# Loading the residual into the accumulator, a third pair of projection weight buffers, and layer norm cut into pieces between projection steps, in a hybrid SSD and MLP block

## The chip, the cores and the metric

The kernel runs on one core of one Trainium2 chip. The metric is the device time of one execution in microseconds (us); lower is better. The engines are named as in the profile: PE is TensorE (PEld its weight loads), DVE is VectorE, ACT is ScalarE, POOL is GpSimd, and SP is the engine whose queue issues the DMAs. One PSUM tile here is 128 partitions by 512 floats.

## The reference

One post-norm layer over 1040 positions (16 meta tokens and 1024 inputs) with 1024 channels. Cut to its last part, which the change touches:

```python
h = layer_norm(concat([meta, x]), ln_in_g, ln_in_b)
...
merged = sigmoid(g_ssm) * (y_ssm @ w_proj_ssm) + sigmoid(g_pool) * (y_pool @ w_proj_pool)
h = layer_norm(ALPHA * h + merged @ w_out, ln1_g, ln1_b)
a, v = split(h @ w_up)                                # 2816 columns each
f = (silu(causal_dwconv(a, conv_w, conv_b)) * v) @ w_down
h = layer_norm(ALPHA * h + f, ln2_g, ln2_b)
return h[:, 16:]
```

ALPHA is 2 to the power of 0.25. All tensors are float32.

## The kernel before

**Arithmetic.** Activations lie transposed, with channels on the partitions and positions in the free dimension. Each float32 operand is split in two by `split` (L117): a rounded copy `hi`, cast by ACT, and the remainder `lo = src - hi`, subtracted by POOL or DVE. A product is three matmuls (`mm3`, L144): hi by hi, hi by lo, lo by hi. A weight tile is 128 by 1024 floats: `loadw` (L128) loads it into `wraw` (two buffers), splits it into `whi` and `wlo` (two buffers each, in the pool `wp`), and the subtraction goes by turns to POOL and DVE in the stretch in question (`lo_pat`).

**The stages around the change, in program order.**

1. Branch projections. For each of eight row blocks m, `gemm(w_ps[m, :, 8:, :], ...)` (L686) multiplies four position chunks CQ (258, 256, 258 and 256 positions); `ev_ssm` (L664) loads the gate `gr` by DMA, multiplies it with the result, adds `acc[:, m]` and splits the sum into `mgh[i]` and `mgl[i]` of chunk i.
2. Output projection. `out_gemm(*idx)` (L712) runs over m and, inside, over the chunks in idx. For each product it loads a piece of the residual `hr` from `h_d` (one buffer) and computes `acc = ALPHA * hr + product` on DVE (L723). Chunks 0 and 2 go first, then 1, then 3.
3. First layer norm. `out_ln(i)` (L725) takes a chunk of `acc`: 86 or 128 positions at a time are transposed on PE into two PSUM tiles, statistics run on DVE (L177), the power of -0.5 on POOL (L184), the normalisation on ACT (L738); the result is transposed back on PE (L744), scaled by DVE and ACT (L746, L748) and written to `h1_d`.
4. `ops_lo` and `ops_hi` (L756, L760) build the operands B11, B21, B22 and T1 to T4 of a seven-product block multiplication from two halves of the positions, each as hi and lo. They overwrite `mgh` and `mgl` and fill `x3h` and `x3l`.
5. Up projection. For f from 0 to 21, `up_weights` (L801) builds weight sums from two `wraw` tiles, `up_steps` runs the seven products for the two subchunks, and `up_act` (L885) applies convolution, SiLU and product and writes `f_d[f]`. The tiles `fpre` and `fv` of even f lie in the pool `pe`, those of odd f in `p6`. The first two f are run in halves, since the second half of the positions is ready later.
6. Down projection. `f_load` (L919) loads `f_d[f]` into `fr`, splits it into `fh` and `fl`; blocks of f (`FBLK`, the first is 0 to 2) are multiplied with `w_down` and added to `acc`. The pool `fp` reuses the memory of `mgs`, `x3s` and `wxs`.
7. Last layer norm, by position chunks 2, 1, 0: transposes, statistics, normalisation on ACT (L1003), then multiply by g2 and add b2 (L1005, L1006) on DVE (a quarter of chunk 0 on POOL), and the output DMA.

**Order.** All instructions are laid out at build time by a scheduler that takes the ready instruction that comes first in the program; `tc.high_priority(offset=n)` moves a block n places forward. Each engine, SP's queue among them, then runs its list strictly in order, and waits at the head of its list. A tile's buffer is reused when all readers of its last content are done. `reuse_waits="tile"` keeps the waits for reused pool memory separate for each tile. `f_d` is one DRAM tile, so its loads and stores are ordered as a whole.

Of the kernel before, what the change touches and what calls it, by code (L numbers as in the profile page):

```python
# [14 lines left out]
P = 128  # L15
# [12 lines left out]
T0 = 12  # L28
# [42 lines left out]
def hybrid_block(ctx: ExitStack, tc, x, w_in, w_dt, pool_w, w_ps, w_pp, w_out, w_up, w_down,  # L71
# [23 lines left out]
    h1_d = dr.tile([KD, P, NT], F32, name="h1_d")  # L95
    f_d = dr.tile([NFF, P, SEQ], F32, name="f_d")
    ac_d = dr.tile([NC, NH, P], F32, name="ac_d")
# [587 lines left out]
    for m in range(KD):  # L685
        gemm(w_ps[m, :, 8:, :], KD, lambda k, a, b: (yb[k][0][:, a:b], yb[k][1][:, a:b]), CQ, ev_ssm(m, True))  # L686
    ybs.close()
    yrs.close()
# [20 lines left out]
    with tc.tile_pool(name="p5", bufs=2, side="right") as p5:  # L709
        hx = {}  # L710

        def out_gemm(*idx):  # L712
            for m in range(KD):
                w = loadw(w_out[m], 8)
                for i in idx:
                    a, b = CQ[i]
                    n = b - a
                    hx[i] = acc[:, :, a:b]
                    ps = gtile()[:, :n]
                    mm3(ps, w, 0, KD, lambda k, a, b: (mgh[i][:, k, :n], mgl[i][:, k, :n]), a, b)  # L720
                    hr = p5.tile([P, 258], F32, tag="hr", name="hr", bufs=1)
                    SY.dma_start(hr[:, :n], h_d[m, :, a + T0:b + T0])
                    V.scalar_tensor_tensor(hx[i][:, m, :], hr[:, :n], ALPHA, ps, ALU.mult, ALU.add)  # L723

        def out_ln(i):  # L725
# [5 lines left out]
            for o in range(0, n, st):  # L731
                pa = [stile("l0"), stile("l1")]
                for k in range(KD):
                    PE.transpose(pa[k // 4][:st, (k % 4) * P:(k % 4 + 1) * P], X[:, k, o:o + st], idn)
                rr = ln_stats(p5, [q[:st] for q in pa], st)
                xn = p5.tile([P, D], F32, tag="xn", name="xn", bufs=3)
                for q in range(2):
                    S.activation(xn[:st, 512 * q:512 * q + 512], pa[q][:st], AF.Identity,  # L738
                                 bias=rr[:st, 1:2], scale=rr[:st, 0:1])
                xs.append((xn, o))  # L740
            for k in range(KD):
                ps = stile("lb")
                for xn, o in xs:
                    PE.transpose(ps[:, o:o + st], xn[:st, k * P:(k + 1) * P], idn[:st, :st])  # L744
                if k % 2:
                    V.tensor_scalar(X[:, k, :n], ps[:, :n], col(PC_1G, k), col(PC_1B, k), ALU.mult, ALU.add)  # L746
                else:
                    S.activation(X[:, k, :n], ps[:, :n], AF.Identity, bias=col(PC_1B, k), scale=col(PC_1G, k))  # L748

            SY.dma_start(h1_d[:, :, a:b].rearrange("k p t -> p k t"), X)  # L750
# [33 lines left out]

        out_gemm(0, 2)
        out_ln(0)
        ops_lo(0)
        out_gemm(1)
        out_ln(2)
        ops_hi(0)  # L790
        out_ln(1)
        ops_lo(1)
        out_gemm(3)
        out_ln(3)
        ops_hi(1)
# [4 lines left out]
    with tc.tile_pool(name="p6", bufs=2, side="right", reuse_waits="tile") as p6:  # L800
# [104 lines left out]
        for f in range(2, NFF):  # L905
            o = up_outs(f)
            up_steps(up_weights(f), *o, [(j, s) for j in range(7) for s in range(2)])
            up_act(f, *o)
    wxs.close()
    x3s.close()  # L910
    mgs.close()
# [3 lines left out]
    fps = ExitStack()  # L915
    fp = fps.enter_context(tc.tile_pool(name="fp", bufs=1, reuse_waits="tile"))
    fops = {}

    def f_load(f):  # L919
        fr = fp.tile([P, SEQ], F32, tag="fr", name="fr", bufs=2)  # L920
        SY.dma_start(fr, f_d[f])
        x, n = ("e", 3) if f in FEARLY else ("", 7)
        th = fp.tile([P, SEQ], F32R, tag="fh" + x, name="fh", bufs=n)
        tl = fp.tile([P, SEQ], F32R, tag="fl" + x, name="fl", bufs=n)
        split(th, tl, fr, lo_eng=V if f < 3 else None)
        fops[f] = th, tl

    with tc.tile_pool(name="p7", bufs=2, reuse_waits="tile") as p6:
        g2 = p6.tile([P, D], F32, name="g2", bufs=1)
        b2 = p6.tile([P, D], F32, name="b2", bufs=1)  # L930
        for f in range(*FBLK[0]):
            f_load(f)
        SY.dma_start(g2, ln2_g.partition_broadcast(P))
        SY.dma_start(b2, ln2_b.partition_broadcast(P))

# [10 lines left out]
        for bi, (f0, f1) in enumerate(FBLK):  # L946
            K = f1 - f0
            fs = [fops.pop(f) for f in range(f0, f1)]
            if f1 < NFF:
                n0, n1 = FBLK[bi + 1]  # L950
                todo = list(range(n0, n1))
                for m in range(KD):
                    if todo:
                        f_load(todo.pop(0))
                    down(m, loadw(w_down[m, :, f0:f1, :], K), K, fs, list(enumerate(CD)), first=bi == 0)
        wcs = ExitStack()
        wcp = pool(wcs, "wcp", 1, side="right")
# [10 lines left out]
        for i in (2, 1, 0):  # L968
# [21 lines left out]
            for o in range(0, b - a, P):  # L990
# [6 lines left out]
                else:  # L997
                    st, pa = pas[o]
                    rr = ln_stats(p6, [], P, st)
                xn = p6.tile([P, D], F32, tag="sa", name="xn", bufs=2)  # L1000
                for q in range(2):
                    sl = slice(512 * q, 512 * q + 512)
                    S.activation(xn[:, sl], pa[q], AF.Identity, bias=rr[:, 1:2], scale=rr[:, 0:1])  # L1003
                    eng = G if i == 0 and o and q else V
                    eng.tensor_mul(xn[:, sl], xn[:, sl], g2[:, sl])  # L1005
                    eng.tensor_add(xn[:, sl], xn[:, sl], b2[:, sl])  # L1006
                    SY.dma_start(out[a + o:a + o + P, sl], xn[:, sl])
# [56 lines left out]
```

## Time and profile before

| | |
|---|---|
| median of 3 runs | 2085.41 us (2081.19 to 2085.63) |
| profiled execution | 2079.03 us |
| its span, first to last instruction | 2077.2 us |
| PE busy | 2002.1 us (96%) |
| DVE busy | 1088.8 us (52%) |
| ACT busy | 780.7 us (38%) |
| POOL busy | 704.1 us (34%) |
| DMA, mean over the span | 103 GB/s |

The profiled execution is 6.4 us below the median of the timed runs. Times in the rows are us from the start of the span. Matmul records overlap, since matmuls are pipelined: a record of 0.28 us can follow the one before by 0.12 us. PEclk 1.00 stands for 2.4 GHz and 0.50 for 1.2 GHz, the two levels of the granted clock.

### The profile page before, as it was taken

Reading aid. Unit: us, or ns where it says so; the run is one execution under the profiler, and the core shown is the slowest. Engines: PE = TensorE matmul, PEld = TensorE weight load, DVE = VectorE, ACT = ScalarE, POOL = GpSimd, SP = SyncE. Lnnn points to the kernel's source line nnn. Section 1 sums busy time; section 2 is a strip of 40 time slices with the busy share of each in tenths; the row PEclk is TensorE's granted clock in tenths of the full one; section 3 lists DMA queues with packets and bytes.
Section 4 is the critical chain, followed back from the end, with each engine's and each line's share of the span. In section 5 each row is a group of like instructions: output and inputs, shape, how many; then the busy total and the mean of one; then the engine's idle time right before and its main releaser. Section 6 shows DMA issues by size and latency. Waiting matters only on the chain.

```text
span 2077.2 us, 33694 instructions
## 1 busy us (share of the span) xinstructions
PE 2002.1 (96%) x13921; PEld 1926.7 (93%) x13921; DVE 1088.8 (52%) x1697; ACT 780.7 (38%) x1146; POOL 704.1 (34%) x447
## 2 busy tenths in 40 slices
PE   7999999999999999999999997889999999899997
PEld 6999999999999999999999997779999999778886
DVE  7847757757755223342233424775554645453337
ACT  4544544635534323232111214554444434322112
POOL 4046657557566310013242323432112121142101
PEclk9999999999999999999999999999999999999998
DMA  6122223232234342225433345452222222343212
GB/s 211 53 81 78 88 79 127 82 112 96 79 114 126 98 142 63 73 78 167 127 121 97 88 123 153 136 174 91 92 72 82 82 72 91 110 159 95 71 54 82
DMA packets 88177, 213.92 MB, mean 103 GB/s; under 512 B 10600, under 2 KB 40136, under 8 KB 88024
## 3 DMA queue, kind: packets, MB, share of 16 engines
q1 hardware_dynamic: 88024, 211.77, 32.1%
q8 instruction: 109, 1.79, 0.4%
q14 instruction: 44, 0.36, 0.1%
HBM read 170.38 MB, written 41.35 MB: 102 GB/s over the span
## 4 chain that ended last, share of the span: by engine, by line
PE 79%; DVE 8%; DMA 5%; POOL 4%; issue 2%; ACT 2%; SPq 0%; POOLq 0%; DVEq 0%; ACTq 0%
PE gps L113 71%; PE sps L113 3%; DMA hr<-h_d 3%; PE yd L113 1%; POOL acb L425 1%; DVE Ct L223 1%; POOL wlo L119 1%; PE yo L113 1%; DMA fr<-f_d 1%; DVE lnst L177 1%; PE st L113 1%; DVE wlo L119 1%; DMA wraw<-in_w_up 1%; DVE acb L426 1%; PE xt L433 1%
## 5 line engine op out<-in xcount | busy, mean ns | idle before, releaser
L113 PE MATMUL gps<-hh,whi 128*128 128x384 f32 (+2 forms) x1536 | 497.8, 324 | 1.1 <-ACT hh L282 1.1
L113 PE MATMUL gps<-hl,whi 128*128 128x384 f32 (+2 forms) x1536 | 493.6, 321 | 4.3 <-POOL hl L285 2.6
L113 PE MATMUL gps<-hh,wlo 128*128 128x384 f32 (+2 forms) x1536 | 490.3, 319 | 0.0
L118 ACT CAST whi<-wraw 128x1024 fp32r<-128x1024 f32 (+3 forms) x246 | 222.2, 905 | 614.8 <-PE gps L113 419.0
L119 POOL TENSOR_TENSOR wlo<-wraw,whi 128x512 fp32r<-128x512 f32 (+1 forms) x85 | 187.7, 2208 | 490.5 <-ACT whi L118 480.4
L113 PEld LDWEIGHTS gps<-hh,whi 128*128 128x128 f32 x1536 | 288.2, 188 | 8.4 <-issue 3.9
L113 PEld LDWEIGHTS gps<-hl,whi 128*128 128x128 f32 x1536 | 288.7, 188 | 7.4 <-POOL hl L285 4.8
L113 PEld LDWEIGHTS gps<-hh,wlo 128*128 128x128 f32 x1536 | 289.5, 189 | 0.8 <-issue 0.8
L119 DVE TENSOR_TENSOR wlo<-wraw,whi 128x1024 fp32r<-128x1024 f32 (+3 forms) x161 | 191.5, 1190 | 148.9 <-ACT whi L118 148.3
L113 PE MATMUL gps<-mgh,wlo 128*128 128x256 f32 (+1 forms) x784 | 225.0, 287 | 10.4 <-POOL wlo L119 7.2
L113 PE MATMUL gps<-mgh,whi 128*128 128x256 f32 (+1 forms) x784 | 224.3, 286 | 4.1 <-ACT whi L118 3.4
L113 PE MATMUL gps<-mgl,whi 128*128 128x256 f32 (+1 forms) x784 | 223.7, 285 | 0.0
L113 PEld LDWEIGHTS gps<-mgh,wlo 128*128 128x128 f32 x784 | 150.2, 192 | 13.0 <-POOL wlo L119 8.9
L113 PEld LDWEIGHTS gps<-mgh,whi 128*128 128x128 f32 x784 | 149.9, 191 | 5.4 <-ACT whi L118 4.5
L113 PE MATMUL gps<-x3h,wlo 128*128 128x258 f32 (+1 forms) x528 | 149.4, 283 | 2.3 <-DVE wlo L119 2.3
L113 PE MATMUL gps<-x3h,whi 128*128 128x258 f32 (+1 forms) x528 | 148.7, 282 | 1.9 <-ACT whi L118 0.9
L113 PEld LDWEIGHTS gps<-mgl,whi 128*128 128x128 f32 x784 | 150.1, 191 | 0.0
L113 PE MATMUL gps<-x3l,whi 128*128 128x258 f32 (+1 forms) x528 | 148.4, 281 | 0.2 <-DVE x3l L119 0.2
L113 PE MATMUL gps<-yh,whi 128*128 128x384 f32 (+3 forms) x448 | 133.6, 298 | 0.0
L113 PE MATMUL gps<-yh,wlo 128*128 128x384 f32 (+3 forms) x448 | 133.4, 298 | 0.0
L113 PE MATMUL gps<-yl,whi 128*128 128x384 f32 (+3 forms) x448 | 133.3, 298 | 0.0
L113 PE MATMUL gps<-fh,whi 128*128 128x512 f32 (+2 forms) x312 | 121.8, 392 | 10.2 <-ACT fh L118 10.2
(256 smaller groups left out, 4184.2 us busy)
## 6 DMA issues: line engine op xcount, KB each, us to landing
wraw<-in_w_in SPq DMA_DIRECT2D x64, 512.0 KB, 3.7
wraw<-in_w_up SPq DMA_DIRECT2D x48, 512.0 KB, 3.5
acb<-ac_d SPq DMA_DIRECT2D x32, 512.0 KB, 4.0
wraw<-in_w_out SPq DMA_DIRECT2D x24, 512.0 KB, 3.7
f_d<-sa SPq DMA_DIRECT2D x22, 512.0 KB, 2.6
fr<-f_d SPq DMA_DIRECT2D x22, 512.0 KB, 3.3
y_d<-xy SPq DMA_DIRECT2D x16, 514.0 KB, 4.2
yr<-y_d SPq DMA_DIRECT2D x16, 514.0 KB, 3.6
```

The costliest lines, as they stand in the source:

```text
L113: PE.matmul(ps, lhsT, rhs, start=start, stop=stop, **kw)
L118: (S.copy if hi_eng is None else hi_eng)(hi, src)
L119: (G if lo_eng is None else lo_eng).tensor_sub(lo, src, hi.bitcast(F32))
L177: V.bn_stats(st[:n, i, :], p)
L223: V.scalar_tensor_tensor(dst, pre[:, j:j + T], cw(j), dst, ALU.mult, ALU.add)
L425: G.tensor_tensor(sg, sg, acc_[:L, c, h0:h1, None].to_broadcast([L, HPG, L]), ALU.subtract)
L426: V.tensor_scalar(sg, sg, 0.0, None, ALU.min)
L433: PE.transpose(px[:L, j * P:(j + 1) * P], xy[:, j, a:b], idn)
```

## The change

The residual is loaded into `acc[:, m]` by one DMA per m right after the last branch projection of m, in place of 32 loads of `hr`; the accumulation reads and writes `acc` in place. The weights of the output projection rotate over three pairs of `whi` and `wlo`, the third in the pool `wx` (its tag is also that of the third pair of the up projection); one subtraction in three goes to POOL and two to DVE. `out_gemm` and `out_ln` become generators, and a written order interleaves the projection steps of chunks 1 and 3 with pieces of the norms of chunks 0, 2 and 1; the norm of chunk 3 comes at the end. `f_d` becomes 22 DRAM tiles. The first three `f_load` calls get a high priority, with their operands in a new pool `fpe` that is opened once `mgs` is closed; the first two load into the memory of `fpre` and `fv` of even f. The loads of g2 and b2 move behind the down projection's first four blocks. In the last layer norm's last chunk, two fused DVE instructions per half replace ACT's normalisation and the multiplication and addition; the mean is taken as it is, without the product with the power (`raw=True`).

```diff
--- before.py
+++ after.py
@@ -93,7 +93,7 @@
     sg_d = dr.tile([KD, P, NT], F32, name="sg_d")
     sp_d = dr.tile([KD, P, NT], F32, name="sp_d")
     h1_d = dr.tile([KD, P, NT], F32, name="h1_d")
-    f_d = dr.tile([NFF, P, SEQ], F32, name="f_d")
+    f_d = [dr.tile([P, SEQ], F32, name=f"f_d{f}") for f in range(NFF)]
     ac_d = dr.tile([NC, NH, P], F32, name="ac_d")
     ea_d = dr.tile([NC, 2, 16, P], F32, name="ea_d")
     rs_d = dr.tile([NG, NT], F32, name="rs_d")
@@ -684,6 +684,7 @@
         mgl.append(mgp.tile([P, KD, 258], F32R, name=f"mgl{i}"))
     for m in range(KD):
         gemm(w_ps[m, :, 8:, :], KD, lambda k, a, b: (yb[k][0][:, a:b], yb[k][1][:, a:b]), CQ, ev_ssm(m, True))
+        SY.dma_start(acc[:, m, :], h_d[m, :, T0:])
     ybs.close()
     yrs.close()
 
@@ -709,18 +710,32 @@
     with tc.tile_pool(name="p5", bufs=2, side="right") as p5:
         hx = {}
 
+        slot = [0]
+
+        def out_w(m):
+            j = slot[0] % 3
+            slot[0] += 1
+            with tc.high_priority(offset=WPRI):
+                raw = wp.tile([P, KD, P], F32, tag="wraw", name="wraw")
+                SY.dma_start(raw, w_out[m])
+                pl, sfx = (wx, "x") if j == 2 else (wp, "")
+                hi = pl.tile([P, KD, P], F32R, tag="whi" + sfx, name="whi")
+                lo = pl.tile([P, KD, P], F32R, tag="wlo" + sfx, name="wlo")
+                split(hi, lo, raw, lo_eng=G if j == 1 else V)
+            return hi, lo
+
         def out_gemm(*idx):
             for m in range(KD):
-                w = loadw(w_out[m], 8)
+                w = out_w(m)
                 for i in idx:
                     a, b = CQ[i]
                     n = b - a
                     hx[i] = acc[:, :, a:b]
                     ps = gtile()[:, :n]
                     mm3(ps, w, 0, KD, lambda k, a, b: (mgh[i][:, k, :n], mgl[i][:, k, :n]), a, b)
-                    hr = p5.tile([P, 258], F32, tag="hr", name="hr", bufs=1)
-                    SY.dma_start(hr[:, :n], h_d[m, :, a + T0:b + T0])
-                    V.scalar_tensor_tensor(hx[i][:, m, :], hr[:, :n], ALPHA, ps, ALU.mult, ALU.add)
+                    o = hx[i][:, m, :]
+                    V.scalar_tensor_tensor(o, o, ALPHA, ps, ALU.mult, ALU.add)
+                yield
 
         def out_ln(i):
             a, b = CQ[i]
@@ -738,6 +753,7 @@
                     S.activation(xn[:st, 512 * q:512 * q + 512], pa[q][:st], AF.Identity,
                                  bias=rr[:st, 1:2], scale=rr[:st, 0:1])
                 xs.append((xn, o))
+                yield
             for k in range(KD):
                 ps = stile("lb")
                 for xn, o in xs:
@@ -746,7 +762,8 @@
                     V.tensor_scalar(X[:, k, :n], ps[:, :n], col(PC_1G, k), col(PC_1B, k), ALU.mult, ALU.add)
                 else:
                     S.activation(X[:, k, :n], ps[:, :n], AF.Identity, bias=col(PC_1B, k), scale=col(PC_1G, k))
-
+                if k % 4 == 3:
+                    yield
             SY.dma_start(h1_d[:, :, a:b].rearrange("k p t -> p k t"), X)
 
         def osplit(name, s, src, lo_eng):
@@ -782,16 +799,32 @@
             V.tensor_sub(t4, xb, t2)
             osplit("T4", s, t4, V)
 
-        out_gemm(0, 2)
-        out_ln(0)
+        def run(g, n=99):
+            for _ in range(n):
+                if next(g, g) is g:
+                    break
+
+        run(out_gemm(0, 2))
+        g1, g3 = out_gemm(1), out_gemm(3)
+        l0, l1, l2, l3 = (out_ln(i) for i in range(4))
+        for todo in ((l0, l0), (l0,), (), (l0,), (l0, l2), (l2,), (l2,), ()):
+            run(g1, 1)
+            for l in todo:
+                run(l, 1)
+        run(l0)
         ops_lo(0)
-        out_gemm(1)
-        out_ln(2)
+        run(g3, 1)
+        run(l2, 1)
+        run(g3, 1)
+        run(l2)
         ops_hi(0)
-        out_ln(1)
+        for todo in ((l1,), (l1,), (l1,), (), (l1,), (l1,)):
+            run(g3, 1)
+            for l in todo:
+                run(l, 1)
+        run(l1)
         ops_lo(1)
-        out_gemm(3)
-        out_ln(3)
+        run(l3)
         ops_hi(1)
 
 
@@ -906,32 +939,36 @@
             o = up_outs(f)
             up_steps(up_weights(f), *o, [(j, s) for j in range(7) for s in range(2)])
             up_act(f, *o)
+    mgs.close()
+
+
+    lo_pat["p"] = (V,)
+    fps = ExitStack()
+    fpe = fps.enter_context(tc.tile_pool(name="fpe", bufs=1, reuse_waits="tile"))
+    fops = {}
+
+    def f_load(f, fr=None):
+        if fr is None:
+            fr = fpe.tile([P, SEQ], F32, tag="fr", name="fr", bufs=2)
+        SY.dma_start(fr, f_d[f])
+        pl, x, n = (fpe, "e", 3) if f in FEARLY else (fp, "", 7)
+        th = pl.tile([P, SEQ], F32R, tag="fh" + x, name="fh", bufs=n)
+        tl = pl.tile([P, SEQ], F32R, tag="fl" + x, name="fl", bufs=n)
+        split(th, tl, fr, lo_eng=V if f < 3 else None)
+        fops[f] = th, tl
+
+    with tc.high_priority(offset=600):
+        for f in range(2):
+            f_load(f, pe.tile([P, NT], F32, tag=("fpre", "fv")[f], name="fre", bufs=1)[:, :SEQ])
     wxs.close()
     x3s.close()
-    mgs.close()
-
-
-    lo_pat["p"] = (V,)
-    fps = ExitStack()
     fp = fps.enter_context(tc.tile_pool(name="fp", bufs=1, reuse_waits="tile"))
-    fops = {}
-
-    def f_load(f):
-        fr = fp.tile([P, SEQ], F32, tag="fr", name="fr", bufs=2)
-        SY.dma_start(fr, f_d[f])
-        x, n = ("e", 3) if f in FEARLY else ("", 7)
-        th = fp.tile([P, SEQ], F32R, tag="fh" + x, name="fh", bufs=n)
-        tl = fp.tile([P, SEQ], F32R, tag="fl" + x, name="fl", bufs=n)
-        split(th, tl, fr, lo_eng=V if f < 3 else None)
-        fops[f] = th, tl
 
     with tc.tile_pool(name="p7", bufs=2, reuse_waits="tile") as p6:
         g2 = p6.tile([P, D], F32, name="g2", bufs=1)
         b2 = p6.tile([P, D], F32, name="b2", bufs=1)
-        for f in range(*FBLK[0]):
-            f_load(f)
-        SY.dma_start(g2, ln2_g.partition_broadcast(P))
-        SY.dma_start(b2, ln2_b.partition_broadcast(P))
+        with tc.high_priority(offset=600):
+            f_load(2)
 
         def down(m, w, K, fs, chunks, first=False):
             for i, (a, b) in chunks:
@@ -953,6 +990,8 @@
                     if todo:
                         f_load(todo.pop(0))
                     down(m, loadw(w_down[m, :, f0:f1, :], K), K, fs, list(enumerate(CD)), first=bi == 0)
+        SY.dma_start(g2, ln2_g.partition_broadcast(P))
+        SY.dma_start(b2, ln2_b.partition_broadcast(P))
         wcs = ExitStack()
         wcp = pool(wcs, "wcp", 1, side="right")
         wc = {m: loadw(w_down[m, :, f0:f1, :], K) for m in range(2)}
@@ -996,14 +1035,18 @@
                     rr = ln_stats(p6, pa, P)
                 else:
                     st, pa = pas[o]
-                    rr = ln_stats(p6, [], P, st)
+                    rr = ln_stats(p6, [], P, st, raw=True)
                 xn = p6.tile([P, D], F32, tag="sa", name="xn", bufs=2)
                 for q in range(2):
                     sl = slice(512 * q, 512 * q + 512)
+                    if i == 0:
+                        V.scalar_tensor_tensor(xn[:, sl], pa[q], rr[:, 1:2], g2[:, sl], ALU.subtract, ALU.mult)
+                        V.scalar_tensor_tensor(xn[:, sl], xn[:, sl], rr[:, 0:1], b2[:, sl], ALU.mult, ALU.add)
+                        SY.dma_start(out[a + o:a + o + P, sl], xn[:, sl])
+                        continue
                     S.activation(xn[:, sl], pa[q], AF.Identity, bias=rr[:, 1:2], scale=rr[:, 0:1])
-                    eng = G if i == 0 and o and q else V
-                    eng.tensor_mul(xn[:, sl], xn[:, sl], g2[:, sl])
-                    eng.tensor_add(xn[:, sl], xn[:, sl], b2[:, sl])
+                    V.tensor_mul(xn[:, sl], xn[:, sl], g2[:, sl])
+                    V.tensor_add(xn[:, sl], xn[:, sl], b2[:, sl])
                     SY.dma_start(out[a + o:a + o + P, sl], xn[:, sl])
         wcs.close()
     fps.close()
```

## Rows read from the trace of the kernel before

**Rows 1.** Stretches: length, busy us (instructions) of PE, PEld, DVE, ACT, POOL; PEclk, DMA.

```profile
1100.00:1201.00 101.00, 101.00 (x826) 101.00 (x826) 39.42 (x74) 21.01 (x39) 28.76 (x35) 1.00 0.35 94
1201.00:1247.10 46.10, 46.10 (x387) 46.10 (x386) 11.32 (x21) 8.81 (x9) 10.18 (x5) 1.00 0.42 124
1247.10:1327.50 80.40, 65.91 (x526) 63.06 (x523) 49.55 (x86) 42.06 (x53) 35.50 (x20) 0.96 0.56 166
1327.50:1394.50 67.00, 52.14 (x358) 47.41 (x358) 48.47 (x67) 33.41 (x52) 22.55 (x12) 0.92 0.46 157
1394.50:1795.00 400.50, 400.24 (x3358) 400.08 (x3358) 218.44 (x322) 170.80 (x301) 72.60 (x40) 1.00 0.24 80
1795.00:1809.70 14.70, 4.42 (x10) 2.98 (x10) 5.67 (x6) 3.94 (x5) 0.00 (x0) 0.66 0.62 205
1809.70:2063.60 253.90, 251.14 (x1202) 211.79 (x1201) 118.93 (x182) 53.89 (x70) 50.98 (x25) 1.00 0.29 93
```

**Rows 2.** Waits of PE, 1247.1 to 1327.5: us in total, times, longest.

```profile
PE l L734 <- ACT xn L738: 6.8, 2, 5.3
PE lb L744 <- ACT xn L738: 3.0, 3, 1.9
PE gps L113 <- POOL wlo L119: 2.4, 3, 1.2
PE gps L113 <- DVE wlo L119: 1.5, 2, 0.8
PE gps L113 <- ACT whi L118: 0.7, 1, 0.7
```

**Rows 3.** Waits of PE, 1327.5 to 1394.5.

```profile
PE gps L113 <- POOL wlo L119: 4.5, 4, 1.7
PE gps L113 <- DVE wlo L119: 4.0, 5, 1.1
PE gps L113 <- ACT whi L118: 3.5, 3, 1.6
```

**Rows 4.** Timeline of DVE: start, duration, instruction, in brackets idle before and releaser.

```profile
1233.50 1.22 DVE L119 TENSOR_TENSOR wlo<-wraw,whi 128x1024 fp32r<-128x1024 f32 x1
...
1252.32 0.42 DVE L723 SCALAR_TENSOR_TENSOR acc<-hr,gps 128x258 f32<-128x258 f32 x1 [4.80 <-DMA hr<-h_d]
...
1305.03 2.49 DVE L119 TENSOR_TENSOR wlo<-wraw,whi 128x1024 fp32r<-128x1024 f32 x1
...
1338.05 0.42 DVE L723 SCALAR_TENSOR_TENSOR acc<-hr,gps 128x256 f32<-128x256 f32 x1 [0.84 <-DMA hr<-h_d]
```

**Rows 5.** Timeline of PE, first product of the up projection.

```profile
1328.68 0.39 PE L113 MATMUL gps<-mgh,wlo 128*128 128x258 f32 x1 [1.23 <-POOL wlo L119]
```

**Rows 6.** Waits of all engines, 1100 to 1201.

```profile
DVE gr L667 <- PE gps L113: 53.3, 31, 3.8
```

**Rows 7.** Chain that ended last, 1770 to 1830, in order of time.

```profile
1777.90 2.89 PE sps L113 x24
...
1798.94 0.33 SPq L894
...
1799.79 5.63 DMA fr<-f_d
```

**Rows 8.** Timelines of DVE and PE around the start of the down projection.

```profile
1778.63 1.23 DVE L893 TENSOR_TENSOR sa<-sa,fv 128x1024 f32<-128x1024 f32 x1
...
1805.29 1.22 PE L113 MATMUL gps<-fh,whi 128*128 128x512 f32 x2 [10.24 <-ACT fh L118]
...
1809.70 0.44 PE L113 MATMUL gps<-fh,whi 128*128 128x512 f32 x1
```

**Rows 9.** Timeline of DVE at the end.

```profile
2066.08 0.27 DVE L181 TENSOR_SCALAR lnmv<-lnmv 128x1 f32<-128x1 f32 x2
...
2068.03 1.36 DVE L1005 TENSOR_TENSOR xn<-xn,g 128x512 f32<-128x512 f32 x2 [0.38 <-ACT xn L1003]
...
2072.30 1.63 DVE L1006 TENSOR_TENSOR xn<-xn,b 128x512 f32<-128x512 f32 x1
```

More of the change, by code (lines that the diff above doesn't have):

```diff
@@ L908, in hybrid_block @@
             up_act(f, *o)
-    wxs.close()
-    x3s.close()
     mgs.close()
@@ L915, in hybrid_block @@
     fps = ExitStack()
-    fp = fps.enter_context(tc.tile_pool(name="fp", bufs=1, reuse_waits="tile"))
+    fpe = fps.enter_context(tc.tile_pool(name="fpe", bufs=1, reuse_waits="tile"))
     fops = {}
-    def f_load(f):
-        fr = fp.tile([P, SEQ], F32, tag="fr", name="fr", bufs=2)
+    def f_load(f, fr=None):
+        if fr is None:
+            fr = fpe.tile([P, SEQ], F32, tag="fr", name="fr", bufs=2)
         SY.dma_start(fr, f_d[f])
-        x, n = ("e", 3) if f in FEARLY else ("", 7)
-        th = fp.tile([P, SEQ], F32R, tag="fh" + x, name="fh", bufs=n)
-        tl = fp.tile([P, SEQ], F32R, tag="fl" + x, name="fl", bufs=n)
+        pl, x, n = (fpe, "e", 3) if f in FEARLY else (fp, "", 7)
+        th = pl.tile([P, SEQ], F32R, tag="fh" + x, name="fh", bufs=n)
+        tl = pl.tile([P, SEQ], F32R, tag="fl" + x, name="fl", bufs=n)
         split(th, tl, fr, lo_eng=V if f < 3 else None)
         fops[f] = th, tl
+    with tc.high_priority(offset=600):
+        for f in range(2):
+            f_load(f, pe.tile([P, NT], F32, tag=("fpre", "fv")[f], name="fre", bufs=1)[:, :SEQ])
+    wxs.close()
+    x3s.close()
+    fp = fps.enter_context(tc.tile_pool(name="fp", bufs=1, reuse_waits="tile"))
     with tc.tile_pool(name="p7", bufs=2, reuse_waits="tile") as p6:
```

## The prediction

> **What bounds the kernel now.** I read the page first: PE is busy for 96% of the span, so a gain has to come from stretches where PE waits or runs at the low clock. Then I cut the span into stretches around the lines that the diff touches. The reader is to see three things [rows 1]. From 1100 to 1247.1, through the end of the branch projections and the projection of chunks 0 and 2, PE is busy without a break, and from 1394.5 to 1795 (f = 2 to 21 of the up projection) for 400.24 of 400.5 us: nothing can be won there. From 1247.1 to 1394.5 PE is idle for 14.5 + 14.9 us, and the mean clock is 0.96 and 0.92. At the change to the down projection PE is busy for 4.4 of 14.7 us, at clock 0.66. Next come the waits of PE in the two halves of the weak stretch [rows 2, 3]: in the first the norm's normalised tile (6.8 + 3.0) costs more than the weights (2.4 + 1.5 + 0.7); in the second the weights cost 4.5 + 4.0 + 3.5.
>
> **How much of the weak stretch is loss.** The pitch of a product with no waits is 46.10 / 387 = 0.119 us [rows 1]. At that pitch the 526 instructions of the first half need 62.6 us and the 358 of the second 42.6; the losses are 80.4 - 62.6 = 17.8 and 67.0 - 42.6 = 24.4 us. (Transposes are a little shorter, so the floor is slightly too high.)
>
> **Residual into the accumulator.** Out go 32 small loads, each holding the only `hr` buffer until DVE has used it. What this costs before is seen at two places. At 1252.32 DVE adds the last piece of chunk 2 after 4.80 us of waiting for `hr`, although PE had left that projection at 1247.1; the first statistics stand behind it in DVE's list, and PE then meets the 5.3 us wait of [rows 2]. At 1338.05 DVE adds the last piece of chunk 3, while PE had begun the up projection by 1328.68 [rows 4, 5]: the last norm starts some 10 us after its products are done. The eight new loads go into SP's list behind the last addition of their m. What is queued behind them are the gates `gr` of the next m; DVE waits there for PE, not for gates (53.3 us in 31 times, [rows 6]), so a gate may come some 1.7 us later (53.3 / 31) before anything moves, and four PSUM tiles stand between DVE and PE. Cost nothing; without that cover at most 8 x 1.7 = 14 us. The new addition reads `acc` instead of `hr`: the same 0.42 us.
>
> **Pieces of the norm between steps, third weight pair.** First half: the waits for the normalised tile, 9.8 us, now have projection steps (24 x 0.119 = 2.9 us each) beside them, and I take them as gone. The 3.4 us of the 17.8 that no wait names are low clock and restarts; I give back 1. Against it, weights are now asked for in 2.9 us plus transposes instead of about 5, so I leave their 4.6 us, pair or no pair, and add 1. First half: 9.8 + 1 - 1 = 10 us (rounded up from 9.8). Second half: the last norm and the operands behind it begin 10 us earlier, so their DVE work no longer falls on the weight splits of the up projection. The weight chain itself (two `wraw` buffers, half as many products for each set of weights) is not touched. I take a quarter of 24.4, 6 us, nearer to the 4.0 us that PE waits for DVE's part than to the whole. Two thirds of the remainders on DVE instead of half: over 24 weights 4 more at 1.22 us [rows 4], 4.9 us of DVE, hidden as DVE is busy for 98 of 147.4 us [rows 1]; without cover it costs 4.9. Bounds for both halves: from below -5 (that cover gone and nothing won), from above 42.2 less the 12.0 us of weight waits in the second half, 30. Taken: 16.
>
> A row bears on the cover: beside a POOL subtraction the same DVE subtraction took 2.49 instead of 1.22 us [rows 4]. The Trainium skill (GPSIMD Engine Reference, 1. Specifications) says that POOL shares its SBUF interfaces with VectorE, with contention for DVE instructions that have two SBUF inputs. The trace agrees, and by that rule a denser stage could be bound by DVE; this is the second rival.
>
> **Early activation tiles.** Before, the chain runs from the last store of `f_d` (1798.94) through a load of 5.63 us, and PE stands idle for 10.24 us from 1795.05 to 1805.29; the products up to 1809.70 then run at half the clock (4.4 us for 2.2) [rows 7, 8]. With one tile for each f, f = 0, 1, 2 no longer wait for that store. Their memory: `fpre` and `fv` of f = 20 are free when its last product ends (1778.63 + 1.23 = 1779.9), and `fpe` takes 32 KB at the place of the first four tiles of `mgs` (33 KB by their shapes), whose last readers, the second products of f = 21, end at 1780.8 [rows 7, 8]. From there 5.6 us for a load, even doubled for three loads side by side, plus a cast and a subtraction (1.2 us each, as the subtraction of the same width in [rows 4]) end by 1794.5, before 1795. Taken: 10.2 + 2.2 = 12.4 us. From below: if the new tiles are not free before the last product of f = 21, the load starts at 1795 instead of 1799.3, 4.2 us. From above one more weight gap, 13.3. The loads of g2 and b2 go behind the fourth block, where PE is busy for 251 of 254 us; nothing.
>
> **Last chunk.** After the variances (2066.35) DVE now runs eight fused instructions of about 0.64 us (the pairs at 2068.03 take 1.36 for two) and two copies: 2066.4 + 0.2 + 5.1 = 2071.7 against 2072.30 + 1.63 = 2073.9 [rows 9]. Taken: 2.3 us; from below 1 (a wait for the power), from above 3.
>
> **Sum.** 10 + 6 + 12.4 + 2.3 = 30.7 us. Against the profiled execution: 2079.0 - 30.7 = 2048.3. That execution is 6.4 us under the median of the timed runs; from the median, 2085.4 - 30.7 = 2054.7. I predict 2054.
>
> **Rivals.**
>
> 1. The early loads don't come early, because memory or the order of SP's list holds them until f = 21 is done. For it: waits for reused memory are inferred by me from shapes. Against it: [rows 7, 8] show the readers done 14 us before. 4.2 instead of 12.4: 2063.
> 2. The weak stretch gains nothing, since DVE and POOL get in each other's way. DVE has 98 + 4.9 us of work there, POOL 58 us [rows 1]; if every POOL stretch halved DVE's rate, DVE would need 103 + 29 = 132 us with no gap, about all that the forecast leaves (147.4 - 16 = 131). Against it: that mean rate is not seen, a part of the overlap is already in the 98. Time: 2085.4 - 14.7 = 2071.
> 3. Nearly everything is won: 30 + 14.7 = 45 us, 2041. For it: in the second half too DVE and POOL are idle for a third of the time; against it: the weight chain of the half sets stays.
> 4. Slower: the pieces themselves become stalls. PE runs its list in order; some 14 pieces now stand between steps, and each needs PSUM tiles that statistics, power and ACT have to free. A step is 2.9 us, while PE's longest wait for such a tile was 5.3 us [rows 2]. From (9.8 + 14.7 + 4) / 14 = 2.0 us for each piece on, the kernel is slower; with half the pieces at 5.3 us it loses 37 - 9.8 = 27 and gains 14.7: 2098. Against it: the longest wait came from a late `hr`, which is gone.
>
> **How the numbers follow.** Forecast 0.55, rival 1 0.10, rival 2 0.17, rival 3 0.13, rival 4 0.05. The likeliest case gives 2054; its own range, with the bounds of the small terms, is 2045 to 2063. For 8 in 10 the range reaches to rivals 2 and 3: 2038 to 2071. A change of under 0.2% (4 us) can't be told from none by a measurement of this kernel. Faster 0.93, within 0.2% 0.03 (part of rivals 2 and 4), slower 0.04.
>
> **What would show it.** Right: PE's wait for `fh` is gone and the clock stays at 1.00 through the change to the down projection; no wait of DVE for `hr`; between the first product of chunk 1 and f = 2 about 131 us instead of 147; DVE's last instruction some 7 to 8 us after PE's last. Wrong: waits of PE for normalised tiles that sum to over 10 us; a mean of DVE's 1024-wide subtractions in that stretch well above 1.4 us; SP's list standing before the loads of f = 0 to 2 until 1795; gates that come late in the branch projections, seen as idle PE there; or new waits in the up projection's 400 us.

## The result, and the profile after

The changed kernel takes 2057.4 us (median of 4 runs, 2055.2 to 2057.5), the kernel before 2083.3 (4 runs, 2080.4 to 2085.6): ratio 0.9874, 95% interval 0.9857 to 0.9891. It is faster by 25.9 us; 2054 was predicted, with 2038 to 2071 as the range. The profiled execution has a span of 2053.4 us against 2077.2, 23.8 us less, and it is this difference that the stages add up to.

Windows of the kernel after, with the columns of [rows 1]. Everything lies 2.0 us later up to the projection of chunks 0 and 2. The third and fourth rows are the halves of the weak stretch, cut where the up projection's first product begins: at 1321.94 us, and at 1326.96 in the kernel before.

```profile
1100.00:1203.00 103.00, 103.00 (x843) 103.00 (x842) 40.77 (x75) 22.08 (x40) 29.70 (x35) 1.00 0.44 128
1203.00:1249.10 46.10, 46.10 (x386) 46.10 (x385) 15.75 (x23) 9.65 (x10) 8.78 (x4) 1.00 0.36 115
1249.10:1321.90 72.80, 62.55 (x520) 59.96 (x520) 54.54 (x89) 40.19 (x52) 23.67 (x16) 0.98 0.43 131
1321.90:1385.90 64.00, 53.82 (x366) 50.46 (x364) 49.44 (x66) 33.74 (x53) 23.00 (x12) 0.87 0.52 173
1386.00:1786.40 400.40, 400.11 (x3358) 400.12 (x3359) 219.72 (x323) 172.54 (x303) 72.58 (x40) 1.00 0.25 84
1786.40:1801.00 14.60, 14.60 (x65) 11.88 (x64) 11.36 (x15) 6.34 (x10) 4.65 (x2) 1.00 0.62 209
```

The weak stretch, from 1247.1 to 1394.4 before, is 136.8 us long instead of 147.3: 10.5 us less, for 884 PE instructions in both. Cut at the first product of the up projection, its halves were 79.9 and 67.4 us (525 and 362 PE instructions) and are now 72.8 and 64.0: 7.1 and 3.4 us less. The 400 us of f = 2 to 21 have not changed. From f = 2 to the first product of the down projection it takes 10.4 us less: PE's idle 10.2 us there are gone, and its clock is 1.00. With them go 2.6 us of the down projection itself. What comes from PE's last transposes on is 2.3 us shorter. The sum, -10.5 - 10.4 - 2.6 - 2.3 + 2.0, is -23.8. The 2.0 us that were lost are there before the branch projections (from 929.0 and 931.0 us the next 272 are alike, 1922 PE instructions without a break), ahead of every line that the diff touches; from 400 to 500 us the granted clock is 0.98 after and 1.00 before. Over the 14 profiled executions of this study the projection of chunks 0 and 2 began between 1199.5 and 1204.6 us, in no order that follows the edits.

Waits of PE over the whole weak stretch (total, times, longest), first the largest of the kernel before, then those of the kernel after:

```profile
PE gps L113 <- POOL wlo L119: 6.9, 7, 1.7
PE l L734 <- ACT xn L738: 6.8, 2, 5.3
PE gps L113 <- DVE wlo L119: 5.5, 7, 1.1
PE gps L113 <- ACT whi L118: 4.3, 4, 1.6
PE lb L744 <- ACT xn L738: 3.8, 4, 1.9
...
PE gps L113 <- DVE wlo L119: 5.5, 5, 2.6
PE lb L760 <- ACT xn L753: 5.3, 5, 2.2
PE gps L113 <- DVE fv L905: 2.8, 1, 2.8
PE l L749 <- ACT xn L753: 2.3, 1, 2.3
PE gps L113 <- POOL wlo L119: 1.9, 2, 1.0
PE gps L113 <- ACT whi L118: 1.4, 1, 1.4
```

The normalised tile `xn`, which was to cost nothing, still costs 5.3 + 2.3 = 7.6 us, 7.2 of them in the first half (before: 6.8 + 3.8 = 10.6, and 9.8 in the first half); the weights, which were to cost what they did, fell from 6.9 + 5.5 + 4.3 = 16.7 to 5.5 + 1.9 + 1.4 = 8.8. So the sum fell, but not where it was to fall.

Timelines of PE, SP, ACT and DVE at the change to the down projection, which answer to [rows 7, 8]:

```profile
1786.31 0.29 PE L113 MATMUL gps<-x3h,wlo 128*128 128x256 f32 x1
1786.43 0.40 PE L113 MATMUL gps<-fh,whi 128*128 128x512 f32 x1
1786.66 0.39 PE L113 MATMUL gps<-fl,whi 128*128 128x512 f32 x1
...
1769.12 2.64 SPq L953 DMA_DIRECT2D fre<-f_d  x2
1771.81 0.42 SPq L927 DMA_DIRECT2D f_d<-sa  x1
1793.95 0.33 SPq L927 DMA_DIRECT2D f_d<-sa  x1
...
1778.63 2.00 ACT L118 CAST fh<-fre 128x1024 fp32r<-128x1024 f32 x2
...
1784.10 2.35 DVE L119 TENSOR_TENSOR fl<-fre,fh 128x1024 fp32r<-128x1024 f32 x2
```

The loads of f = 0 and 1 leave SP at 1769.1, ahead of the last two stores of `f_d`; the remainders are ready at 1786.45, while the first product that reads one begins at 1786.66. The first product of the down projection follows the last of the up projection without a gap. DVE is only just in time: its two subtractions end 0.2 us before a remainder is first read. (The loads of g2 and b2, which stand behind four blocks in the program, leave SP at 1786.5 all the same, with the first product of the down projection, and cost PE nothing.)

Timelines of PE's last transposes and DVE's last instructions, which answer to [rows 9]:

```profile
2042.13 1.10 PE L1020 MATMUL l<-idn,acc 128*128 128x128 f32 x6 [1.47 <-DVE acc L981]
...
2044.86 1.40 DVE L1043 SCALAR_TENSOR_TENSOR xn<-l,lnrr,g 128x512 f32<-128x512 f32 x2
2048.82 1.41 DVE L1044 SCALAR_TENSOR_TENSOR xn<-xn,lnrr,b 128x512 f32<-128x512 f32 x2
```

DVE ends 7.0 us after PE; the eight fused instructions take 1.40 us for two, 0.1 more than was reckoned.

### The profile page after: what moved, and what is told of

Same layout as the page of the kernel before. It is cut to its first block, busy times and chain, and to the rows that moved or that the text cites. A ratio compares the mean times of both kernels' runs of the same rounds, so it can differ in the third digit from the quotient of the medians.

```text
span 2053.4 us, 33613 instructions
## 1 busy us (share of the span) xinstructions
PE 2000.8 (97%) x13921; PEld 1928.9 (94%) x13921; DVE 1096.1 (53%) x1703; ACT 776.7 (38%) x1142; POOL 686.5 (33%) x441
## 5 line engine op out<-in xcount | busy, mean ns | idle before, releaser
L119 POOL TENSOR_TENSOR wlo<-wraw,whi 128x512 fp32r<-128x512 f32 (+1 forms) x81 | 174.6, 2156 | 484.7 <-ACT whi L118 475.7
L119 DVE TENSOR_TENSOR wlo<-wraw,whi 128x1024 fp32r<-128x1024 f32 (+3 forms) x165 | 194.7, 1180 | 150.8 <-ACT whi L118 150.1
L113 PE MATMUL gps<-fh,wlo 128*128 128x512 f32 (+2 forms) x312 | 121.4, 390 | 0.5 <-DVE wlo L119 0.5
```

The lines of the kernel that those rows point to most:

```text
L113: PE.matmul(ps, lhsT, rhs, start=start, stop=stop, **kw)
L119: (G if lo_eng is None else lo_eng).tensor_sub(lo, src, hi.bitcast(F32))
```

## The experiments

Three questions were open: which of the three edits carries the weak stretch, why the normalised tile still costs PE 7.6 us, and what brings the early tiles early. Each kernel is the changed one with the edit shown; the times stand beside the kernel before on the same chip. "Stretch" is the length of the weak stretch in the profiled execution, measured from PE's end of the projection of chunks 0 and 2 to f = 2. In five executions of kernels whose program is the same there (the changed one twice, and the three below that alter only the early tiles) it is 136.8 to 138.0 us; a difference under 2 us is taken as nothing. The ratios of the total times are too wide to order the runs of 2059.6 to 2060.6 us below, or to part them surely from the changed kernel, whose second set of runs has 0.9892 (0.9875 to 0.9908); what is said of them rests on the stretch, one profiled execution each.

**Two pairs of weight buffers.** With two pairs every other remainder goes to POOL again, instead of every third.

```
-            j = slot[0] % 3
+            j = slot[0] % 2
```

> The changed kernel with two pairs of weight buffers for the output projection instead of three (POOL and DVE by turns again); all else as changed. The weak stretch, from the last product of chunks 0 and 2 to f = 2 of the up projection, took 147.4 us before and 136.9 after; PE's waits for weights in it fell from 17.0 to 8.8 us, those for normalised tiles and their transposes only from 10.6 to 8.5. Theory A (the third pair carries the gain of this stretch): the weight waits come back, 8 us, stretch about 145, total about 2065. Rivals B (the late residual was the cost) and C (the pieces between the steps carry it): stretch within 2 us of 137, total 2057 to 2059.

2059.6 us (before 2079.5), ratio 0.9905 (0.9890 to 0.9919); stretch 140.6, 3.8 over that of the changed kernel. PE's waits in it:

```profile
PE gps L113 <- POOL wlo L119: 7.3, 5, 2.4
PE gps L113 <- ACT whi L118: 5.4, 4, 2.7
PE gps L113 <- DVE wlo L119: 3.9, 7, 0.9
PE lb L760 <- ACT xn L753: 2.6, 4, 1.0
PE l L749 <- ACT xn L753: 1.4, 1, 1.4
```

The weights are back at 16.6 us, as before the change, and the normalised tile is down to 4.0. At 140.6 us neither theory's figure (145; within 2 of 137) came. With the written order kept, the halved waits for weights belong to the pair, or to the share of POOL that it changes.

**The residual by small loads again.**

```
-        SY.dma_start(acc[:, m, :], h_d[m, :, T0:])
...
-                    o = hx[i][:, m, :]
-                    V.scalar_tensor_tensor(o, o, ALPHA, ps, ALU.mult, ALU.add)
+                    hr = p5.tile([P, 258], F32, tag="hr", name="hr", bufs=1)
+                    SY.dma_start(hr[:, :n], h_d[m, :, a + T0:b + T0])
+                    V.scalar_tensor_tensor(hx[i][:, m, :], hr[:, :n], ALPHA, ps, ALU.mult, ALU.add)
```

> The changed kernel with the residual loaded again in 32 pieces through the one small buffer; all else as changed. Theory A (third pair): stretch within 2 us of 137, total 2057 to 2059. Theory B (late residual): additions wait for loads again (17 us of DVE waits before), the first and last norm start 5 and 10 us late, stretch 145 or more, total 2065 to 2068. My prediction gave the residual no separate sum; it saw it as the cause of 5.3 of the 9.8 us of waits for normalised tiles and of the late last norm, so it expects at least 5 us.

2067.1 us (before 2079.5), ratio 0.9940 (0.9924 to 0.9957); stretch 150.8, longer than the 147.3 of the kernel before. DVE's largest wait there, and PE's, are

```profile
DVE acc L737 <- DMA hr<-h_d: 16.6, 7, 4.1
...
PE gps L113 <- DVE lnmv L179: 6.3, 1, 6.3
```

With one buffer for the residual, DVE stands in front of a load seven times, and pieces of a norm stand in its list too: once a product waits 6.3 us for a norm's statistics. Without the residual in the accumulator, the pieces and the pair lose 3.5 us.

**Whole norms between whole projections.** The order of before, with the residual and the pair kept.

```
-        for todo in ((l0, l0), (l0,), (), (l0,), (l0, l2), (l2,), (l2,), ()):
-            run(g1, 1)
...
+        run(out_ln(0))
+        ops_lo(0)
+        run(out_gemm(1))
+        run(out_ln(2))
+        ops_hi(0)
+        run(out_ln(1))
+        ops_lo(1)
+        run(out_gemm(3))
+        run(out_ln(3))
+        ops_hi(1)
```

> The changed kernel with whole norms between whole projections in the order of before (chunks 0 and 2; norm 0; chunk 1; norm 2; norm 1; chunk 3; norm 3), residual and third pair as changed. Theory C (the pieces carry the gain): stretch back to 145 or more, total 2065. Theories A and B: within 3 us of 137, total 2057 to 2060, since the scheduler takes ready products between the parts of a norm anyway, as the trace of before shows it doing with chunk 1.

2060.1 us (before 2079.5), ratio 0.9907 (0.9892 to 0.9922); stretch 141.2. PE waits 9.2 + 5.9 + 2.0 = 17.1 us for weights and 6.0 for normalised tiles. Here too the stretch lies between the two theories (145 or more; within 3 of 137). The third pair and POOL's smaller share are in place, and the waits for weights are not halved: that takes the written order as well.

**The residual alone**, with two pairs and the order of before (the two edits above together; early tiles and last chunk kept).

> The changed kernel with both the third pair and the written order taken back, so that of the weak stretch's three edits only the residual in the accumulator is left (early tiles and last chunk as changed). So far the stretch took 147.3 us before, 136.7 with all three, 140.6 without the pair, 141.2 without the order and 150.8 without the residual. If the three add up: 140.6 + 141.2 - 136.7 = 145.1 us, total about 2065. Rival (the residual alone carries most, pair and order overlap): 142 us or less, total 2061.

2060.6 us (before 2078.6), ratio 0.9908 (0.9892 to 0.9925); stretch 140.5. A sum of separate gains had to give 145.1, so that reckoning is refuted. PE's waits in the stretch:

```profile
PE gps L113 <- POOL wlo L119: 11.2, 7, 2.6
PE gps L113 <- ACT whi L118: 6.3, 6, 2.5
PE gps L113 <- DVE wlo L119: 3.4, 5, 0.9
PE l L749 <- ACT xn L753: 2.1, 2, 1.4
PE lb L760 <- ACT xn L753: 0.6, 2, 0.3
```

This is the step that the prediction gave to the pieces: with whole norms in the old places, the normalised tile costs 2.7 us instead of 10.6. The residual does it by itself. The weights then rise from 16.7 to 20.9, and the net gain is 6.8 us, 3.4 in each half (76.5 and 64.0 us, with some transposes more in the first). Pair and order add 3.7 together (2.5 to 3.7 over the five executions above), and neither adds anything without the other (140.6 with the order alone, 141.2 with the pair alone, 140.5 with neither).

**The early tiles late**, as in the kernel before: in the late pool and without high priority; the split of `f_d` in 22 tiles kept.

```
-            fr = fpe.tile([P, SEQ], F32, tag="fr", name="fr", bufs=2)
+            fr = fp.tile([P, SEQ], F32, tag="fr", name="fr", bufs=2)
...
-    with tc.high_priority(offset=600):
-        for f in range(2):
-            f_load(f, pe.tile([P, NT], F32, tag=("fpre", "fv")[f], name="fre", bufs=1)[:, :SEQ])
...
-        with tc.high_priority(offset=600):
-            f_load(2)
+        for f in range(3):
+            f_load(f)
```

> The changed kernel with the early tiles taken back (operands of f = 0, 1, 2 in the late pool, no high priority), but with one DRAM tile for each f and g2, b2 loaded late. If the early memory carries the 12.9 us of the change to the down projection: PE idle there again, about 10 us less what the separate DRAM tiles save (they let a load start when the last product ends instead of after the last store, 4 us): total 2057 + 8 to 9 = 2066. Rival (the one DRAM tile was the whole cause): total 2057 to 2060.

2067.8 us (before 2079.5), ratio 0.9945 (0.9930 to 0.9960). SP's and PE's timelines:

```profile
1789.16 0.33 SPq L927 DMA_DIRECT2D f_d<-sa  x1
1789.53 8.64 SPq L952 DMA_DIRECT2D fr<-f_d  x4
...
1795.39 1.22 PE L113 MATMUL gps<-fh,whi 128*128 128x512 f32 x2 [10.11 <-ACT fh L118]
```

All of the gap is back, and the loads stand right behind the last store although they read other tiles of `f_d`. The split alone saves nothing. The trace shows no wait of the first loads themselves: SP waits 1.5 us for DVE before the store, and they follow it at once, 4.2 us after the up projection's last product. So at that moment their place in SP's list holds them, a place that the scheduler gave them at build time.

**One tile for `f_d` again**, early memory and priority kept.

```
-    f_d = [dr.tile([P, SEQ], F32, name=f"f_d{f}") for f in range(NFF)]
+    f_d = dr.tile([NFF, P, SEQ], F32, name="f_d")
```

> The changed kernel with f_d as one DRAM tile again, the early memory and the priority kept. Taking the early memory back alone left PE idle for 10.4 us, with the loads issued right behind the last store in SP's list. If the one DRAM tile too is enough to hold the loads behind the last store: PE idle 10 us, total 2057 + 12 = 2069, and the prediction's step needs both edits. Rival (the memory alone decides): no idle time, total as changed.

2055.1 us (before 2078.6), ratio 0.9886 (0.9872 to 0.9901), and there is no gap. On SP:

```profile
1766.44 2.64 SPq L953 DMA_DIRECT2D fre<-f_d  x2
1769.13 0.42 SPq L927 DMA_DIRECT2D f_d<-sa  x1
```

The loads pass the last two stores with a single tile too, so it is not right that with one tile loads and stores are ordered as a whole, as the section on the kernel before has it. What the early loads need is a place that is free early; the 22 tiles do nothing for them.

**The early tiles without priority.**

```
-    with tc.high_priority(offset=600):
+    with nullcontext():
         for f in range(2):
```

(and the same for f = 2.)

> The changed kernel with the early memory kept and the high priority of the three loads taken back. Priority and memory together removed 10.4 us of idle time; one DRAM tile for f_d made no difference. If SP's order is what holds the loads: without priority they stand behind the last store and PE is idle for about 10 us. Rival (the memory holds them): the loads start as early as with priority, no idle time.

2052.1 us in its one run; there is no gap, and the loads of f = 0 and 1 leave at 1766.0 and 1768.7. So the early memory is enough, with neither the priority nor the split. Late memory with the priority kept was not run; whether it would bring the loads ahead of the store is open.

**No remainder of the output projection on POOL.**

```
-                split(hi, lo, raw, lo_eng=G if j == 1 else V)
+                split(hi, lo, raw, lo_eng=V)
```

> The changed kernel with all remainders of the output projection's weights on DVE, so that POOL has only the powers of the norms and two operand remainders in the stretch. Theory D (the norm's chain is long because its power stands behind a 2.4 us subtraction on POOL; DVE waited 8.6 us for powers, up to 3.2): PE's waits for normalised tiles fall from 7.6 to 4 us or less and the stretch from 136.7 to 134. Rival E (DVE, busy for 104 of 137 us, is the limit): 5 more subtractions of 1.2 us on it lengthen the stretch to 138 or more.

2049.0 us (before 2078.6), ratio 0.9858 (0.9843 to 0.9873); stretch 130.5, 6.3 us under the changed kernel. The row that bears on it in the changed kernel: the timelines of POOL, then of DVE.

```profile
1276.54 2.37 POOL L119 TENSOR_TENSOR wlo<-wraw,whi 128x1024 fp32r<-128x1024 f32 x1
1278.87 0.55 POOL L184 TENSOR_TENSOR lnrr<-lnmv,mhalf 86x1 f32<-86x1 f32 x1
...
1279.45 0.15 DVE L186 SCALAR_TENSOR_TENSOR lnrr<-lnmv,lnrr 86x1 f32<-86x1 f32 x1 [3.17 <-POOL lnrr L184]
```

The power of one element a partition takes 0.55 us but stands behind a subtraction of 2.37, and DVE stands idle for 3.17. In the stretch DVE waits for powers for 8.6 us, the longest 3.2; without the subtractions it is

```profile
DVE lnrr L186 <- POOL lnrr L184: 5.4, 9, 0.7
```

and PE waits 2.6 + 1.0 = 3.6 us for normalised tiles instead of 7.6. That DVE's own work is the limit, the rival, is refuted: DVE has more to do (105.9 us of 130.5, against 104.0 of 136.9), and the stretch is shorter. How much of the 6.3 us comes by way of the power, and how much by DVE being held up less (the section on the hardware), the run doesn't separate.

**A third `wraw` buffer**, in the memory of `fv`.

```
+                if j == 2:
+                    raw = pe.tile([P, NT], F32, tag="fv", name="wraw3", bufs=1)[:, :D].rearrange("p (k c) -> p k c", c=P)
```

> The changed kernel with a third buffer for the unsplit weights of the output projection as well (in the memory of fv, which is idle then). Theory F (the third pair is fed too late because only two loads can be under way): PE's waits for weights fall from 8.8 us to 5 or less, stretch 133 to 135, total 2054. Rival (the casts and subtractions on ACT and DVE are late, not the loads): stretch within 1.5 us of 136.7.

2055.8 us (before 2078.6), ratio 0.9889 (0.9875 to 0.9904); stretch 135.9. No effect that can be told from scatter, and the waits for weights didn't fall (10.6 us, 8.8 in the changed kernel): more room for loads doesn't shorten them, which is the rival's case.

**The changed kernel again, and two that build on the best:** the first weights' remainders of f = 0 and 1 of the up projection on DVE too, and this with the third `wraw` buffer.

```
-                split(hi, lo, raw, lo_eng=G if j == 1 else V)
+                split(hi, lo, raw, lo_eng=V)
...
-            split(w1[0], w1[1], r1, lo_eng=G)
+            split(w1[0], w1[1], r1, lo_eng=V if f < 2 else G)
```

> The changed kernel itself, unedited, on the chip of the other three, as their measure: weak stretch 136.7 us within 1.5, ratio to before about 0.987.

> All remainders of the output projection's weights on DVE (stretch 130.5 us), and of the first two f of the up projection the remainder of the first weight tile on DVE too instead of POOL. In that stretch DVE still waits 5.6 us for POOL's subtraction before it may overwrite the tile, and PE 2.5 us for it. Theory D2 (POOL's 2.4 us subtractions lengthen every chain here): stretch 127 to 129. Rival E (DVE, 106 of 130 us busy, is near its limit): 130 or more.

> As the run before with the first two f on DVE, and the third buffer for unsplit weights as well. Alone that buffer shortened the stretch by 1 us (within the scatter of about 1.3 that repeated layouts show). If loads are now the next limit: 2 us or more below the run without it; if casts and DVE are: no difference.

Beside 2078.4 us of the kernel before: the changed kernel 2055.6, ratio 0.9892 (0.9875 to 0.9908); with the remainders on DVE 2048.3, 0.9855 (0.9840 to 0.9870); with the buffer too 2047.2, 0.9850 (0.9835 to 0.9866). The stretches are 137.7, 129.0 and 128.7. Both beat the changed kernel, by 7 to 8 us; between them, and against the kernel with only the output projection's remainders moved, nothing can be told apart.

## Why the prediction held, and which term was mis-sized

The forecast held: 30.7 us were predicted and 25.9 came between the medians. Of what was to show it, four things came: no wait of PE for `fh`, the clock at 1.00 there, no wait of DVE for the residual, and DVE's end 7.0 us after PE's. The fifth, a stretch of 131 us, is 136.8. That the total comes so near owes something to luck: the weak stretch won 5.5 us less than was reckoned and 2.0 went ahead of the change, while the kernel before, beside which it is measured, came out 2.1 us faster than the median that the prediction started from.

- **Early activation tiles: 12.4 us, measured 10.4 + 2.6 = 13.0.** Gap and low clock went as reckoned. Of the two reasons given, one is wrong: "With one tile for each f, f = 0, 1, 2 no longer wait for that store" is neither needed (one tile: no gap) nor enough (split alone: the whole gap). The early memory is what it takes, and part of it is free sooner than I took it to be: the two loads leave 17.3 and 15.0 us before the end of the up projection, where I had put 14.2. Rival 1, in which memory or SP's list holds them, is refuted for the change as made; without the early pool the loads do stand in SP's list until after the last store. The reserve at the end was read rightly as small (0.5 us predicted; the subtraction pair ends 0.2 us before the first use of a remainder).
- **Last chunk: 2.3 us, measured 2.3.**
- **Residual: cost of the eight loads nothing, and so it was** (PE busy for 103.00 of 103.00 us while they are issued). Its cover was read too well: besides the waits for PE in [rows 6], the same view of before has 2 waits of DVE for gates, 4.5 us; the kernel after has 5, 11.6 us, and its second profile 1, 2.2 us. None reached PE. The gain that the prediction gave it is in the second half (6 us; 3.4 came, and the residual alone gives nearly all of it), and in the first it gave the gain to the pieces. There too the residual carries much: alone about 3.4 of 7.1 us; and with it left out the stretch with pieces and pair is longer than before.
- **Weak stretch: 10 + 6 = 16 us, measured 7.1 + 3.4 = 10.5. This is the term that was mis-sized.** The step that failed is that the 9.8 us of waits for normalised tiles "now have projection steps ... beside them, and I take them as gone", and that the weights cost as much as before, "pair or no pair". In the first half 7.2 of the 9.8 us stayed; the weights, put at 4.6 + 1, fell to 2.6, and the rest of the loss, put at 2.4, came to about 1. So the first half came to 7.1 us by errors that partly cancel. Measured over the whole stretch:

| | norm tile, us | weights, us | PE idle in all, us | stretch, us |
|---|---|---|---|---|
| before | 10.6 | 16.7 | 29.4 | 147.3 |
| residual alone | 2.7 | 20.9 | 23.9 | 140.5 |
| residual and pieces | 4.0 | 16.6 | 24.7 | 140.6 |
| residual and pair | 6.0 | 17.1 | 23.6 | 141.2 |
| all three | 7.6 | 8.8 | 20.4 | 136.8 |
| all three, no remainder on POOL | 3.6 | 7.8 | 16.4 | 130.5 |

(Idle is a window's length less PE's busy time.) The late residual, not the whole norm, made the norm's tiles late. What the pieces and the pair together then do is trade: weights halve, and the norm's chain, now among the subtractions of the projection's weights on POOL and DVE, grows again. So rival 2 held in part: the two engines do get in each other's way, but at a cost of some 6 us, the gain of taking the remainders off POOL, and not of the whole stretch. Its observable came true too, weakly: the 32 two-input instructions of 1024 or 1032 elements on DVE in the stretch take 49.7 us, 1.55 each (1.33 before; 1.45 to 1.54 in the other four executions with the same program there), where a mean well above 1.4 was to count against the forecast.

- **The cover of the remainders on DVE held.** Four more of 1.22 us were costed at nothing; eight more are even a gain.
- **Rival 4**, pieces that become stalls, fits the run with the late residual: with its small loads back a product waits 6.3 us for a norm's statistics, and the stretch is 3.5 us longer than before (pieces and pair are not told apart there). With the residual in the accumulator the stretch is never longer than before. Rival 3, nearly all won, stays out of reach even with POOL's subtractions gone: 147.3 - 128.7 = 18.6 us of the 30.

Left open is what the third pair's buffers are worth apart from the smaller share of POOL that came with them. POOL has 13, 10 and 5 weight subtractions of 1024 elements in the stretch with two pairs, three pairs and none of the projection's own, and the stretch grows by (140.6 - 136.8) / 3 = 1.3 and (136.8 - 130.5) / 5 = 1.3 us for each: the share alone could explain all of the pair's effect. That the two quotients agree so well is chance (with the 137.7 us of the second execution they are 1.0 and 1.4), it holds only with the written order (without it three subtractions fewer gain nothing: 140.5 and 141.2), and the next four, those of f = 0 and 1, are worth less (1.5 us together). Three pairs with every other remainder on POOL would tell; it was not run.

## What to carry to other kernels

A wait is put down to the operand that comes last: take one away, and the time goes to the next in line, so two edits on one stretch are sized together, by the idle time and the runs with one of them, not by adding named waits. Before a stage is interleaved, look for what is late at its entrance (here a residual with one buffer), and for small links of a dependent chain that share an engine with long, movable work (a power of 0.55 us behind subtractions of 2.4). Where loads stand behind a store in the queue's list, ask first whether they could have had their buffers sooner, before splitting the tensor that both touch.

## What the runs showed of the hardware

**Of two subtractions on DVE and POOL at once, the one that starts second waits.** Timelines of DVE and POOL of the kernel after:

```profile
1310.64 1.23 DVE L119 TENSOR_TENSOR x3l<-acc,x3h 128x1032 fp32r<-128x1032 f32 x1
...
1312.92 3.40 DVE L119 TENSOR_TENSOR x3l<-acc,x3h 128x1032 fp32r<-128x1032 f32 x1
...
1312.83 2.39 POOL L119 TENSOR_TENSOR wlo<-wraw,whi 128x1024 fp32r<-128x1024 f32 x1 [6.83 <-ACT whi L118]
...
1352.76 4.51 DVE L119 TENSOR_TENSOR x3l<-acc,x3h 128x1024 fp32r<-128x1024 f32 x2
...
1353.14 3.04 POOL L119 TENSOR_TENSOR wlo<-wraw,whi 128x1024 fp32r<-128x1024 f32 x1 [4.32 <-ACT whi L118]
...
1261.86 2.37 POOL L119 TENSOR_TENSOR wlo<-wraw,whi 128x1024 fp32r<-128x1024 f32 x1
...
1261.90 2.34 DVE L186 SCALAR_TENSOR_TENSOR lnrr<-lnmv,lnrr 86x1 f32<-86x1 f32 x1 [0.66 <-POOL lnrr L184]
```

The same instruction on DVE takes 1.23 us alone and 3.40 when it starts 0.09 us behind POOL's of 2.39: 2.17 us more, nearly the whole of POOL's time; [rows 4] show 2.49 for 1.22. When DVE starts first (the first of the two at 1352.76), POOL's takes 3.04. The Trainium skill (Trainium Architecture — The Big Picture, What this means for kernel authors) calls the shared ports of the two engines an exclusive lock and not a split of bandwidth; the trace agrees, with 1.23 + 2.17 against 2.39. It strikes single instructions: the 13 weight remainders of 1024 elements on DVE in that stretch have a mean of 1.22 us, the six `x3l` one of 1.94 and the two of L788 one of 2.48; in the kernel before the last two kinds took 1.22 each.

It also strikes small ones: the last row is a link of the norm's chain, one element a partition, that takes 2.34 us behind POOL's subtraction where its other nine in the stretch take 0.15 or 0.16. So POOL's subtractions hold that chain in two ways, ahead of the power on POOL and beside the next step on DVE. With no remainder of the projection on POOL none of the ten takes over 0.16.

**The clock doesn't follow the idle time.** In the kernel after PE is idle for 10.3 of 72.8 us in the first half of the weak stretch and for 10.2 of 64.0 in the second; the granted clock is 0.98 and 0.87, means over its two levels of 2.4 and 1.2 GHz. Windows of the kernel after:

```profile
1346.00:1354.00 8.00, 5.20 (x34) 4.99 (x34) 8.00 (x8) 4.26 (x5) 3.68 (x2) 0.80 0.56 176
1354.00:1362.00 8.00, 6.30 (x28) 5.71 (x27) 6.63 (x7) 2.83 (x5) 2.75 (x2) 0.56 0.46 156
```

PE was busy for 5.20 of 8 us, the clock fell within them, and PE then ran mostly at the lower level, 28 instructions in 6.30 us. The change took 9 us of idle time out of the stretch, yet its mean clock is 0.93, as against 0.94 before: in these traces what the clock costs has to be read, and can't be reckoned from the idle time saved.
